# The passage from the output projection to the MLP: turning the first token tile early, with ordered engines

## The chip, the cores and the metric

One NeuronCore of a Trainium2 chip runs the whole program. The metric is the device time of one execution in microseconds, as the median of several runs. The matrix engine (TensorE) appears in the profile as PE for matmuls and PEld for its weight loads, VectorE as DVE, ScalarE as ACT, GpSimd as POOL, and SyncE, which issues most transfers, as SP.

## The reference

The reference is one layer of a transformer-like block on 256 tokens of width 2048. Three mixing branches (two kinds of attention and a recurrent one) are gated, summed and projected; then a two-layer MLP follows. What matters here is the end of the first half and the beginning of the second:

```python
m = g_a * (y_a @ w_branch_a) + g_b * (y_b @ w_branch_b) + g_c * (y_c @ w_branch_c)
x = x + rms_norm(m @ w_out, norm_mix_post)
hdn = square(relu(rms_norm(x, norm_mlp_pre) @ w_mlp_up))      # 2048 -> 8192
x = x + rms_norm(hdn @ w_mlp_down, norm_mlp_post)             # 8192 -> 2048
```

All is in float32 from end to end.

## The kernel before

**Precision by parts.** A float32 product is made of three products of a reduced form: each operand is split into a high part (a rounded copy) and a low part (the rest), and high x high, low x high and high x low are summed in PSUM. A weight tile of 128 x 1024 therefore goes through three stages: a transfer from DRAM into a buffer `raw` (three buffers), a copy by ACT to `whi` (line 144) and a subtraction by DVE to `wlo` (line 145), each with three buffers in the pool `wpool`. `wsplit` does the two operations, `wraw` the transfer, and `wnext` keeps `AHEAD` (one) further weights split ahead in the list `wq`. Activations are packed the same way, high part beside low part, in tiles named `pk` of 128 x 512.

**Token form and column form.** In the output projection the tokens stand on the PSUM partitions. `tok` computes, for one block of 512 output columns, two PSUM tiles, one for each half of the tokens (token tile 0 and 1). It goes through eight weight tiles, which I call steps; a step holds two slices of 128 of the inner dimension and makes six matmuls of 512 columns for each token tile. Its parameter `lag` says for how many of the last steps the second token tile is put off: `prod` computes token tile 0 for those steps first, `tok` hands out the first PSUM tile, and then does the kept steps for token tile 1. In the MLP's first layer the hidden columns stand on the partitions. A unit is 128 hidden columns; it takes two weight tiles (halves), and in each half eight matmuls with the high part of the weight over 512 columns (high and low parts of all 256 tokens) and eight with the low part over 256 columns.

**The passage.** Four column blocks (`for g in range(4)`) of the output projection give `m @ w_out`. Each PSUM tile is squared and summed by ACT (line 888) and multiplied with the norm's gain by DVE (line 886) into `mg`. The fourth block completes the mean square; two small operations on POOL (lines 861 and 862) make the norm's factor `r2` from it, and `add_mixed` (line 878, DVE) adds the scaled result to `x1`. The MLP needs `x1` the other way around: `turned` (line 907) turns it with 128 x 128 transposes on PE, two token tiles side by side in a PSUM tile `mps`, and `split` (lines 225 and 226) makes the 16 packed tiles `upk2`, with the next norm's gain as scale. In the fourth block `lag` is 4. Transposes of token tile 0 come after the last product of token tile 1, a few PSUM tiles ahead of those of token tile 1.

**The MLP.** The hidden dimension is worked in four quarters `q`. For the first, 16 units (`up`) run by themselves. Their results are finished by `post` (copy, add, relu, square) and brought by `forms` to the operands `fm` of the down product, which for the first three quarters is written with seven block products instead of eight (`down`; lines 1069 to 1071 are its three matmuls, line 963 loads its weights into `raw2`, line 1033 adds such weights on DVE and line 1036 by a transfer of POOL's). Units of the next quarter are mixed between these products in a list `work`, which `drive` runs through: it prepares the next item's weights, issues an item's matmuls, and then the posts of the item before.

**What sets the order.** Within a stretch marked with `tc.manual_schedule(engines=...)` the named engines execute their instructions in the order in which the program writes them. Elsewhere a planner that estimates durations orders each engine's instructions before the program runs. In either case each engine runs its own stream in a fixed order, and semaphores hold an instruction until its inputs are there and its buffer is free. In the kernel before, PE alone has a manual stretch, in the mixing branches, which ends ahead of the third gate; the output projection and the MLP are planned. SBUF pools are opened and closed as a stack; a new pool takes over the memory of a closed one as its tiles come free.

Of the kernel before, what the change touches and what calls it, by code (L numbers as in the profile page):

```python
# [17 lines left out]
T = 256  # L18
D = 2048
# [30 lines left out]
def hybrid_block(ctx, tc, xt, x, gains, params, consts, lora, gup, wst, out):  # L50
# [90 lines left out]
    def wsplit(raw):  # L141
        hi = wpool.tile([128, HALF], F32R, tag="whi", name=nm("whi"), bufs=3)
        lo = wpool.tile([128, HALF], F32R, tag="wlo", name=nm("wlo"), bufs=3)
        A.activation(hi, raw, AF.Copy)  # L144
        V.tensor_tensor(lo, raw, hi.bitcast(F32), ALU.subtract)  # L145
# [31 lines left out]
    def tok(pks, lag=1):  # L177
# [31 lines left out]
        for hl, k0 in kept:  # L209
            prod(hl, k0, 1)  # L210
            tick()
        yield ps[1]
# [630 lines left out]

    def fm():
        return p2.tile([128, 7, 128], F32R, tag="fm", name=nm("fm"), bufs=16)

    def gain(n, tiles):

        t = [a.bitcast(F32) for a in tiles]
# [15 lines left out]
    g2, loads = gain(0, [fm().rearrange("p a b -> p (a b)")[:, 0:512] for _ in range(4)])  # L865
# [13 lines left out]

    r2, sum2 = [], []  # L880
    ss2 = cpool.tile([128, 2, 4], F32, name="ss2")
    for g in range(4):
        gs = slice(512 * g, 512 * g + 512)
        for tt, ps in enumerate(tok(mpk, 4 if g == 3 else 1)):
            def gained():
                V.tensor_tensor(mg[tt][:, gs], ps, g2[g], ALU.mult)

            A.activation(junk(), ps, AF.Square, accum_out=ss2[:, tt, g:g + 1])
            if g < 3:
                gained()  # L890
                if g == 2:
                    sum2.append(rstd_of(ss2[:, tt, :], EPS, None))
                continue
            r2.append(rstd_of(ss2[:, tt, :], EPS, sum2[tt]))
            if tt == 0:
                gained()
                for c in range(0, D, 512):
                    add_mixed(0, c, 512)
            else:
                pend = gained  # L900
    upk2 = []
    ss3 = cpool.tile([128, 2, 4], F32, name="ss3")
    trs = []

    def turned(k2, tt):
        for i in range(2):
            PE.transpose(trs[k2 // 2][:, i * T + tt * 128:i * T + tt * 128 + 128],
                         x1[tt][:, (k2 + i) * 128:(k2 + i) * 128 + 128], C("ident"))

    for k2 in range(0, KT, 2):  # L910
        while len(trs) < min(k2 // 2 + 4, 8):
            trs.append(mps())
            turned(2 * len(trs) - 2, 0)
        if k2 == 8:
            pend()
# [388 lines left out]
```

## Time and profile before

| | |
|---|---|
| median of 3 runs | 1560.79 us (1556.21 to 1565.39) |
| profiled execution | 1562.27 us |
| its span, first to last instruction | 1560.5 us |
| mean granted TensorE clock | 0.991 |
| busy: PE, PEld | 98%, 81% of the span |
| busy: DVE, ACT, POOL | 74%, 58%, 6% |
| read from HBM | 279.77 MB, 181 GB/s over the span |
| last output-projection block begins | 829.96 us |
| down products begin | 951.16 us |

The times of a profile are of that one execution, from its first instruction on. Matmuls are pipelined, so the start-to-start distance of weight loads (PEld) tells more of PE's pace than the duration of one matmul. A row of the timeline merges equal instructions that follow one another; a bracket at its end says how long the engine was idle before it and what ended that wait. Idle time of an engine other than PE costs nothing by itself here.

### The profile page before, as it was taken

The numbers are of one execution on the slowest core, as the hardware profiler recorded it, in microseconds if no ns is written. First come the engines' busy times: TensorE is split into PE (matmuls) and PEld (weight loads), VectorE is DVE, ScalarE is ACT, GpSimd is POOL, SyncE is SP. The second block draws the span as 40 slices with busy tenths as digits, with TensorE's granted clock in tenths as the row PEclk, the third lists the DMA queues.
The fourth block names the chain that finished last, engine by engine and source line by source line (L and its number), as shares of the span: only waits on it lengthen the run. The fifth ranks groups of instructions, "written<-read, shape, count | busy, mean of one in ns | idle before, by whom it ended". The sixth has DMA issues, their size and how long they took to land.

```text
span 1560.5 us, 22381 instructions
## 1 busy us (share of the span) xinstructions
PE 1524.2 (98%) x8318; PEld 1265.7 (81%) x8318; DVE 1157.1 (74%) x1566; ACT 907.9 (58%) x1369; POOL 88.5 (6%) x146
## 2 busy tenths in 40 slices
PE   7999999999999999999999999999999999999997
PEld 6888887887887787788887888888888877888885
DVE  7765568896558896645555778789988899888855
ACT  7565367545466554644444766567766676666542
POOL 0030001100001100000000000000000000000000
PEclk9999999999999998999999999999999999999999
DMA  7645554455445553355695557798888888887764
GB/s 242 206 159 176 162 165 150 138 190 189 135 144 179 174 164 96 125 180 188 228 306 164 171 188 201 216 266 254 242 257 250 230 236 239 263 253 232 214 200 136
DMA packets 101197, 308.50 MB, mean 198 GB/s; under 512 B 10080, under 2 KB 12512, under 8 KB 101088
## 3 DMA queue, kind: packets, MB, share of 16 engines
q1 hardware_dynamic: 91344, 280.66, 55.1%
q0 software_dynamic: 6912, 25.17, 8.7%
q8 instruction: 65, 1.06, 0.3%
q10 hardware_dynamic: 2832, 1.24, 0.3%
q14 instruction: 44, 0.36, 0.1%
HBM read 279.77 MB, written 2.10 MB: 181 GB/s over the span
## 4 chain that ended last, share of the span: by engine, by line
PE 66%; issue 10%; DVE 10%; DMA 9%; ACT 4%; POOL 0%; ACTq 0%; SPq 0%; POOLq 0%; DVEq 0%
PE gps L204 27%; PE gps L160 15%; PE gps L164 8%; DMA raw<-raw 5%; PE gps L189 5%; DVE wlo L145 5%; DMA raw<-in_wst_dram 4%; ACT whi L144 2%; PE gps L166 1%; PE mps L1069 1%; PE mps L1071 1%; PE mps L1070 1%; PE gps L1071 1%; PE gps L1069 1%; PE gps L1070 1%
## 5 line engine op out<-in xcount | busy, mean ns | idle before, releaser
L145 DVE TENSOR_TENSOR wlo<-raw,whi 128x1024 fp32r<-128x1024 f32 x590 | 716.1, 1223 | 272.4 <-ACT whi L144 254.4
L144 ACT ACTIVATE whi<-raw 128x1024 fp32r<-128x1024 f32 x590 | 618.2, 1055 | 342.0 <-PE gps L204 153.8
L160 PE MATMUL gps<-pk,whi 128*128 128x512 f32 x1501 | 386.2, 395 | 2.1 <-ACT whi L144 1.0
L160 PEld LDWEIGHTS gps<-pk,whi 128*128 128x128 f32 x1501 | 278.2, 189 | 62.4 <-issue 5.8
L204 PE MATMUL gps<-whi,pk 128*128 128x512 f32 x1144 | 293.8, 395 | 0.4 <-ACT whi L144 0.4
L204 PEld LDWEIGHTS gps<-whi,pk 128*128 128x128 f32 x1144 | 213.5, 189 | 47.0 <-issue 1.3
L164 PEld LDWEIGHTS gps<-pk,wlo 128*128 128x128 f32 x1608 | 220.1, 191 | 16.0 <-DVE wlo L145 0.7
L164 PE MATMUL gps<-pk,wlo 128*128 128x256 f32 x1608 | 225.9, 283 | 0.1
L204 PE MATMUL gps<-wlo,pk 128*128 128x512 f32 x572 | 159.8, 397 | 0.4 <-DVE wlo L145 0.4
L204 PEld LDWEIGHTS gps<-wlo,pk 128*128 128x128 f32 x572 | 107.3, 190 | 24.2 <-DVE wlo L145 1.1
L991 ACT ACTIVATE tmp<-gps 128x256 f32<-128x256 f32 x64 | 24.6, 384 | 90.7 <-PE gps L166 90.7
L1069 PE MATMUL mps<-whi,fm 128*128 128x512 f32 x192 | 76.1, 396 | 0.8 <-ACT whi L144 0.7
L1071 PE MATMUL mps<-wlo,fm 128*128 128x512 f32 x192 | 75.5, 393 | 0.4 <-DVE wlo L145 0.2
L1070 PE MATMUL mps<-whi,fm 128*128 128x512 f32 x192 | 75.0, 391 | 0.0
L1036 POOL DMA_DIRECT2D raw<-raw x48 | 41.9, 873 | 554.2 <-DVE raw L1033 313.2
L189 PE MATMUL gps<-whi,pk 128*128 128x512 f32 x264 | 71.3, 393 | 0.0
L1071 PE MATMUL gps<-wlo,fm 128*128 128x512 f32 x144 | 57.2, 397 | 2.4 <-DVE wlo L145 2.1
L1033 DVE TENSOR_TENSOR raw<-raw,raw 128x1024 f32<-128x1024 f32 x48 | 58.7, 1223 | 1.0
L189 PEld LDWEIGHTS gps<-whi,pk 128*128 128x128 f32 x264 | 49.2, 188 | 11.2 <-issue 0.7
L1069 PE MATMUL gps<-whi,fm 128*128 128x512 f32 x144 | 56.8, 395 | 1.4 <-ACT whi L144 1.4
L1070 PE MATMUL gps<-whi,fm 128*128 128x512 f32 x144 | 56.5, 392 | 0.0
L204 PE MATMUL gps<-whi,fm 128*128 128x512 f32 x208 | 51.4, 389 | 0.0
(294 smaller groups left out, 1551.7 us busy)
## 6 DMA issues: line engine op xcount, KB each, us to landing
raw<-in_wst_dram SPq DMA_DIRECT2D x518, 512.0 KB, 4.4
raw<-raw POOLq DMA_DIRECT2D x48, 512.0 KB, 6.7
x<-in_x_dram SPq DMA_DIRECT2D x8, 256.0 KB, 6.5
out_dram<-x SPq DMA_DIRECT2D x8, 256.0 KB, 2.8
x<-in_xt_dram SPq DMA_DIRECT2D x3, 512.0 KB, 7.3
fm<-in_gains_dram SPq DMA_DIRECT2D x4, 256.0 KB, 5.5
pk<-in_gains_dram SPq DMA_DIRECT2D x4, 256.0 KB, 4.5
con<-in_consts_dram SPq DMA_DIRECT2D x1, 576.0 KB, 7.8
```

Source lines behind the costliest of these rows:

```text
L144: A.activation(hi, raw, AF.Copy)
L145: V.tensor_tensor(lo, raw, hi.bitcast(F32), ALU.subtract)
L160: PE.matmul(ps, hi[:, i * 128:i * 128 + 128], pks[i], start=first and i == 0, stop=False)
L164: PE.matmul(ps[:, 0:T], lo[:, i * 128:i * 128 + 128], pks[i][:, 0:T], start=False, stop=False)
L189: PE.matmul(ps[tt], pks[k][:, c:c + 128], w[:, (k - k0) * 512:(k - k0) * 512 + 512], start=k == 0 and part == 0 and w is hl[0], stop=w is ...
L204: PE.matmul(ps[tt], pks[k][:, c:c + 128], w[:, (k - k0) * 512:(k - k0) * 512 + 512], start=k == 0 and part == 0 and w is hl[0], stop=False)
L991: A.activation(b, ps[0][:, T:2 * T], AF.Copy)
L1033: V.tensor_tensor(R[a], R[a], R[b], ALU.add)
L1036: G.dma_start(out=R[a], in_=R[b], accum_op=ALU.add)
L1069: PE.matmul(Q[f], a, w, start=d == 0 and i == 0, stop=False)
L1070: PE.matmul(Q[f], b, w, start=False, stop=False)
L1071: PE.matmul(Q[f], a, wl, start=False, stop=d == 3 and i == 1)
```

## The change

It has five parts.

1. Token tile 0 is turned early. In the fourth block `lag` goes from 4 to 6, and `tok` takes a list `mid` of functions to call between the kept steps of token tile 1. After the fourth of the six, two PSUM tiles of token tile 0 are turned and cut (`early`), after the fifth a third, after the sixth the last.
2. Token tile 0's share of three units. The six weights of the units 0 to 2 are split ahead into `uw`. `part` does the matmuls with the high weight parts for one token tile alone, high and low tokens in one matmul as two runs of 128 columns; `rest` does those with the low weight parts for both. Token tile 0's parts stand before and between the transposes of token tile 1.
3. More split weights ahead. The lookahead grows block by block (`ahead` 1, 3, 6, 9), up to the six weights of `uw` (`top`). From the eighth step on most split weights go into a pool `op` of 18 further tiles `kw`; the pool closes after the three units, and only then the pool `p3` (for `fm`, `raw2` and `sfm`) opens. `raw` keeps its three buffers.
4. Order. From the fourth block to the end of the first quarter's units PE, ACT, DVE and POOL run in written order; PE alone does so from there to the last down product's beginning.
5. Token tile 1's gain multiplication follows directly on its square, and `add_mixed` works on 512 columns for it as well. `cut` splits 128 columns at a time. The MLP's squares for its second norm go from the units 0 to 7 to the units 4 to 11.

```diff
-    def wsplit(raw):
-        hi = wpool.tile([128, HALF], F32R, tag="whi", name=nm("whi"), bufs=3)
-        lo = wpool.tile([128, HALF], F32R, tag="wlo", name=nm("wlo"), bufs=3)
+    def wsplit(raw, n=None):
+        hl = home[0](n) if home[0] else None
+        hi, lo = hl or (wpool.tile([128, HALF], F32R, tag=t, name=nm(t), bufs=3) for t in ("whi", "wlo"))
...
-        while len(wq) < 1 + AHEAD and wpos[0] < wst.shape[0]:
-            wsplit(wraw())
+        while len(wq) < 1 + ahead[0] and wpos[0] < top[0]:
+            wsplit(wraw(), wpos[0] - 1)
...
-        for hl, k0 in kept:
+        for i, (hl, k0) in enumerate(kept):
             prod(hl, k0, 1)
             tick()
+            if i < len(mid):
+                mid[i]()
...
+    def roomy(n):
+        if n - wo < 8 or (n - wo) % 12 < 3:
+            return None
+        return [op.tile([128, HALF], F32R, tag="kw", name=nm("kw"), bufs=18) for _ in range(2)]
+
+    home[0], top[0] = roomy, wo + 38
...
+    def turn(tt, b):
+        trs[tt, b] = mps()
+        for i in range(4):
+            PE.transpose(trs[tt, b][:, 128 * i:128 * i + 128],
+                         x1[tt][:, 512 * b + 128 * i:512 * b + 128 * i + 128], C("ident"))
...
+    def part(j, half, tt):
+        for i in range(8):
+            o, u = (t.rearrange("p (a t) -> p a t", a=2)[:, :, 128 * tt:128 * tt + 128] for t in (gp[j], upk2[8 * half + i]))
+            PE.matmul(o, uw[2 * j + half][0][:, i * 128:i * 128 + 128], u, start=tt == half == i == 0, stop=False,
+                      skip_group_check=True)
...
+    mid = [lambda: None] * 3 + [lambda: early(0, 1), lambda: early(2)]
+    order = tc.manual_schedule(engines={mybir.EngineType.PE, mybir.EngineType.Activation, mybir.EngineType.DVE, mybir.EngineType.Pool})
     for g in range(4):
...
+        if g == 3:
+            order.__enter__()
+        for tt, ps in enumerate(tok(mpk, 6, mid) if g == 3 else tok(mpk)):
             A.activation(junk(), ps, AF.Square, accum_out=ss2[:, tt, g:g + 1])
+            if g == 3:
+                r2.append(rstd_of(ss2[:, tt, :], EPS, sum2[tt]))
+            V.tensor_tensor(mg[tt][:, gs], ps, g2[g], ALU.mult)
...
+            if g == 3 and tt == 0:
                 for c in range(0, D, 512):
                     add_mixed(0, c, 512)
+        ahead[0] = (3, 6, 9, AHEAD)[g]
+    uw = [wq.pop(0) for _ in range(6)]
+    gp = [gps() for _ in range(3)]
+    home[0], top[0] = None, wst.shape[0]
+    early(3)
+    for j in range(3):
+        part(j, 0, 0)
+    for b in range(4):
+        add_mixed(1, 512 * b, 512)
+    part(0, 1, 0)
+    turn(1, 0)
+    part(1, 1, 0)
+    turn(1, 1)
+    cut(1, 0, 1)
+    turn(1, 2)
+    part(2, 1, 0)
+    turn(1, 3)
+    cut(1, 2, 3)
+    for _ in range(1 + AHEAD):
+        wsplit(wraw())
...
-    for j in range(KT):
+    for j in range(3):
+        rest(j, 0)
+    for half in range(2):
+        for j in range(3):
+            part(j, half, 1)
+            if half:
+                rest(j, 1)
+                hidden(0, j, gp[j])
+    po.close()
...
+    forms(0, 0)
+    for j in range(3, KT):
         work.extend(up(0, j))
...
     drive()
+    order.__exit__(None, None, None)
+    order = tc.manual_schedule(engines={mybir.EngineType.PE})
+    order.__enter__()
```

`early(b, ...)` turns the named quarters of token tile 0 and cuts them; `cut` copies with the gain as scale on ACT (all high parts first) and subtracts on DVE; `hidden` is the old `post` under a new name.

More of the change, by code (lines that the diff above doesn't have):

```diff
@@ L863, in rstd_of @@
         return r
-    g2, loads = gain(0, [fm().rearrange("p a b -> p (a b)")[:, 0:512] for _ in range(4)])
+    g2, loads = gain(0, [op.tile([128, 512], F32, name=nm("g2")) for _ in range(4)])
     x1 = [p2.tile([128, D], F32, tag="x1", name=nm("x1"), bufs=2) for _ in range(2)]
@@ new lines, in cut @@
+    def cut(tt, *bs):
+        for low in range(2):
+            for b in bs:
+                for i in range(4):
+                    k = 4 * b + i
+                    if len(upk2) == k:
+                        upk2.append(pk())
+                    hi, lo = (upk2[k][:, c + 128 * tt:c + 128 * tt + 128] for c in (0, T))
+                    src = trs[tt, b][:, 128 * i:128 * i + 128]
+                    if low:
+                        V.scalar_tensor_tensor(lo, src, P("g3", k), hi.bitcast(F32), ALU.mult, ALU.subtract)
+                    else:
+                        A.activation(hi, src, AF.Copy, scale=P("g3", k))
@@ new lines, in part, with rest @@
+    def part(j, half, tt):
[3 more added lines that the diff above has]
+                      skip_group_check=True)
+    def rest(j, half):
+        for i in range(8):
+            PE.matmul(gp[j][:, 0:T], uw[2 * j + half][1][:, i * 128:i * 128 + 128], upk2[8 * half + i][:, 0:T],
+                      start=False, stop=half == 1 and i == 7, skip_group_check=True)
@@ L897, in hybrid_block @@
+            if g == 2:
+                sum2.append(rstd_of(ss2[:, tt, :], EPS, None))
+            if g == 3 and tt == 0:
                 for c in range(0, D, 512):
                     add_mixed(0, c, 512)
-            else:
-                pend = gained
-    upk2 = []
-    ss3 = cpool.tile([128, 2, 4], F32, name="ss3")
[L903 to L915, printed above, removed]
-        add_mixed(1, 128 * k2, 256)
-        turned(k2, 1)
-        for i in range(2):
-            u = pk()
-            split(trs[k2 // 2][:, i * T:i * T + T], u, P("g3", k2 + i))
-            upk2.append(u)
+        ahead[0] = (3, 6, 9, AHEAD)[g]
+    assert len(wq) == 6
+    uw = [wq.pop(0) for _ in range(6)]
@@ L976, in hybrid_block, with hidden @@
     hid, fmh, fml = {}, {}, {}
+    def hidden(q, j, ps):
+        b, t = tmp(), tmp()
+        A.activation(b, ps[:, T:2 * T], AF.Copy)
+        V.tensor_tensor(t, ps[:, 0:T], b, ALU.add)
+        A.activation(t, t, AF.Relu)
+        if j % 2 == 0:
+            hid[q, j // 2] = pk().bitcast(F32).rearrange("p (s t) -> p s t", s=4)
+        h = hid[q, j // 2]
+        A.activation(h[:, 0:4:3] if j % 2 == 0 else h[:, 1:3], t.rearrange("p (s t) -> p s t", s=2), AF.Square)
+        if q == 0 and 4 <= j < 12:
+            A.activation(junk(), x1[j % 2][:, 512 * (j // 2 - 2):512 * (j // 2 - 2) + 512], AF.Square,
+                         accum_out=ss3[:, j % 2, j // 2 - 2:j // 2 - 1])
+        if q == 0 and j in (12, 13):
+            e = cpool.tile([128, 2], F32, name=nm("eps4"))
+            V.tensor_reduce(e[:, 0:1], ss3[:, j % 2, :], AX.X, ALU.add)
+            V.tensor_scalar(e[:, 0:1], e[:, 0:1], 1.0 / D, EPS, ALU.mult, ALU.add)
+            V.tensor_tensor(e[:, 1:2], e[:, 0:1], e[:, 0:1], ALU.mult)
+            V.tensor_scalar(e[:, 1:2], e[:, 1:2], EPS, None, ALU.mult)
+            eps4.append(e[:, 1:2])
     def up(q, j):
@@ L1153, in hybrid_block @@
     drive()
+    order.__exit__(None, None, None)
     hp = [hp[k] for k in range(KT)]
```

58 lines of the change are left out of this document (20 added, 38 removed).

## The prediction

> **What bounds the kernel now.** I read the page first, then the table of windows around the passage, then the timeline there. In the windows the columns after the stretch are its length, the busy time of PE, PEld, DVE, ACT and POOL with counts, the granted clock, the DMA share and GB/s.
>
> ```profile
> PE 1524.2 (98%) x8318; PEld 1265.7 (81%) x8318; DVE 1157.1 (74%) x1566; ACT 907.9 (58%) x1369; POOL 88.5 (6%) x146
> 829.96:846.28 16.32, 16.32 (x73) 13.51 (x72) 7.64 (x11) 5.88 (x8) 0.00 (x0) 1.00 0.58 194
> 846.28:852.57 6.29, 6.06 (x26) 4.38 (x25) 3.90 (x5) 4.46 (x6) 1.42 (x2) 1.00 0.30 101
> 852.57:878.54 25.97, 23.18 (x128) 18.50 (x129) 21.96 (x46) 19.48 (x47) 1.37 (x2) 0.93 0.37 118
> 857.46:860.87 3.41, 2.91 (x9) 2.03 (x10) 3.37 (x9) 3.41 (x11) 0.00 (x0) 0.50 0.01 2
> 951.16:1461.66 510.50, 504.31 (x2546) 422.53 (x2545) 448.77 (x511) 337.40 (x469) 41.20 (x48) 1.00 0.84 243
> ```
>
> TensorE bounds nearly everything: it is busy 1524.2 of 1560.5 us. So an edit is worth only the holes that it closes in PE's stream. The passage has some: in 852.57 to 878.54 PE is busy for 23.18 of 25.97 us at a mean clock of 0.93, and the 3.41 us from 857.46 ran at 0.50. These three windows hold all that the turning edits can win. The later window, the down products, is the other place that the edit touches.
>
> The next rows, of the timeline, give start and duration; a bracket is idle time and what ended it.
>
> ```profile
> 764.12 0.42 PEld L835 LDWEIGHTS mps<-ident,m 128*128 128x128 f32 x4 [0.40 <-PE gps L189]
> 764.51 1.46 PEld L204 LDWEIGHTS gps<-whi,pk 128*128 128x128 f32 x7
> ...
> 829.96 1.77 PEld L204 LDWEIGHTS gps<-whi,pk 128*128 128x128 f32 x8
> 832.68 1.77 PEld L204 LDWEIGHTS gps<-whi,pk 128*128 128x128 f32 x8
> 840.84 0.87 PEld L189 LDWEIGHTS gps<-whi,pk 128*128 128x128 f32 x4
> ...
> 849.39 0.60 ACT L888 ACTIVATE junk<-gps 128x512 f32<-128x512 f32 x1 [0.72 <-PE gps L189]
> 851.13 0.56 POOL L862 TENSOR_TENSOR rs<-rs,cst 128x1 f32<-128x1 f32 x1
> 851.72 2.74 DVE L878 SCALAR_TENSOR_TENSOR x<-mg,rs,x 128x512 f32<-128x512 f32 x4 [0.21 <-POOL rs L862]
> 852.54 0.42 PEld L907 LDWEIGHTS mps<-ident,x 128*128 128x128 f32 x4 [0.62 <-PE gps L189]
> 853.69 0.82 POOL L861 TENSOR_SCALAR rs<-ss,ssum 128x1 f32<-128x1 f32 x1 [2.01 <-ACT junk L888]
> 855.18 1.67 DVE L878 SCALAR_TENSOR_TENSOR x<-mg,rs,x 128x256 f32<-128x256 f32 x4 [0.72 <-POOL rs L862]
> 855.72 1.62 PE L907 MATMUL mps<-ident,x 128*128 128x128 f32 x8 [1.88 <-DVE x L878]
> ...
> 878.53 1.80 PEld L160 LDWEIGHTS gps<-pk,whi 128*128 128x128 f32 x8
> 884.12 1.80 PEld L160 LDWEIGHTS gps<-pk,whi 128*128 128x128 f32 x8
> ```
>
> A full output-projection step is 832.68 - 829.96 = 2.72 us (12 matmuls, 0.227 each), half a step (one token tile) 1.36. Four transposes take 764.51 - 764.12 = 0.39. An MLP unit takes 884.12 - 878.53 = 5.59, so its 16 narrow matmuls (256 columns) take (5.59 - 16 x 0.227) / 16 = 0.123 each. From the square of a finished tile (849.39) over POOL's two operations and the adds to the first transpose (852.54) is 3.15 us. In the old order the second tile's chain has little beside it: PE waits 1.88 us for its add.
>
> **The change part by part.** Passage: unit 3 starts at 878.53. The last column block (g == 3) starts at 829.96. Without holes it needs 8 x 2.72 = 21.8 us, the 32 transposes 8 x 0.39 = 3.1 and three units 16.8: 871.6. The old holes and the slow clock are therefore 6.9 us together.
>
> The new order adds PE work: in `part`, 48 wide matmuls become 96 narrow ones, 96 x 0.123 - 48 x 0.227 = 0.9 us. No row has a matmul whose columns lie in two runs of 128. I take the contiguous narrow price, the nearest row; if each cost half a wide one (0.114) nothing would be added, and at a wide one's price 10.9. Ideal end 872.5, **at most 6.0 us won**.
>
> Does tile 0 arrive in time? Step 24 and 25 run whole and six steps for tile 0 alone, so tile 0 ends at 829.96 + 5.44 + 8.16 = 843.6. Four half steps of tile 1 carry PE to 849.0. Its chain of 3.15 would give the first transpose at 846.9, 2.1 us early. But ACT now runs in written order, and `tok` has written the splits of weights 30 to 37 ahead of tile 0's square. All eight must land first. That supply decides:
>
> ```profile
> L144 ACT ACTIVATE whi<-raw x14: 1059/1061/1063, 811.4 to 847.6; 128x1024 fp32r<-128x1024 f32 x14
> L145 DVE TENSOR_TENSOR wlo<-raw,whi x15: 1224/1226/1228, 809.9 to 849.7; 128x1024 fp32r<-128x1024 f32 x15
> DMA to landing us min/median/max: 3.2/4.2/5.2
> ...
> 787.42 0.43 SPq L963 DMA_DIRECT2D raw<-in_wst_dram  x1
> 797.56 1.06 ACT L144 ACTIVATE whi<-raw 128x1024 fp32r<-128x1024 f32 x1 [0.20 <-DMA raw<-in_wst_dram]
> 808.64 0.43 SPq L963 DMA_DIRECT2D raw<-in_wst_dram  x1
> 829.93 1.06 ACT L144 ACTIVATE whi<-raw 128x1024 fp32r<-128x1024 f32 x1 [0.22 <-PE gps L189]
> ```
>
> `raw` still has three buffers. A buffer is held from issue to landing (median 4.2 in 811 to 850), through whi (1.06) and wlo (1.23): 6.5 us for three loads, 2.16 each, whatever number of kw buffers follows. That is faster than PE eats whole steps (2.72), slower than half steps (1.36). Steps from 0: whi at 829.93 waited for PE to finish step 23, whose buffer it takes, so it is step 26; twelve splits earlier, 797.56 is step 14, which waited on its load. From there the ring runs freely: step 37 is 23 loads later, 797.6 + 23 x 2.16 = 847.3, its whi ends at 848.4. Square and chain then give the first transpose at 848.4 + 3.15 = 851.5, against PE free at 849.0: a hole of 2.5, and 0.3 more as the second chunk's add (2.74 / 4 = 0.69) outlasts its four transposes. So **2.8 us of stall**. Bounds from the landings: at 3.2 a cycle is 5.5, whi ends at 840.8, no stall; at 5.2 a cycle is 7.5, whi ends at 856.2, stall 10.7. I take the median's row. The old loads of the down weights (L963, 787.42 to 808.64) leave this stretch, since their pool now opens later; they are wanted only from 951 and cost nothing there.
>
> The old half clock at 857.46 followed a hole of 1.88; the new one is longer, so I count one: 3.41 x 0.5 = 1.7 us. Passage: 6.0 - 2.8 - 1.7 = **1.5 us won**. The Trainium skill, "TensorE: Matmul & The Clock Gate", section "Part 1: The HAM clock gate", says that an idle window of some 3.4 us drops PE to half rate; here the stretch at 0.50 is 3.41 us long, but the hole was shorter than that window. By the page's words a hole of 2.8 would cost no clock, and the passage would win 3.2, a case inside the forecast's own range.
>
> Behind that, little is late. Tile 1's chain, 3.15 plus four new `cut` subtractions ahead of its adds, has `turn(0,3)` and 32 narrow matmuls beside it (0.39 + 32 x 0.123 = 4.3).
>
> ```profile
> L225 ACT ACTIVATE pk<-mps,par 128x256 fp32r<-128x256 f32 x16 | 6.8, 472 | 4.5 <-DVE pk L226 2.5 <-PE mps L907 2.0
> L226 DVE SCALAR_TENSOR_TENSOR pk<-mps,par,pk 128x256 fp32r<-128x256 f32 x16 | 7.1, 478 | 0.6 <-ACT pk L225 0.5
> L1016 DVE TENSOR_TENSOR sfm<-pk,sfm 128x128 f32<-128x128 f32 x3 | 0.9, 289 | 0.1
> ```
>
> `cut` makes 32 operations of 128 columns per engine instead of 16 of 256. At the nearest small row (0.289) that is 32 x 0.289 - 16 x 0.478 = 1.6 us more on DVE and about the same on ACT, between nothing and the full 7.6; it lies under the 17.5 us of the three units. If that cover went, all 1.6 would show. In the rest of the units DVE and ACT now follow written order too:
>
> ```profile
> 878.54:951.16 72.62, 72.62 (x419) 63.91 (x417) 51.67 (x76) 45.85 (x78) 0.71 (x1) 1.00 0.60 189
> ```
>
> They are busy 51.67 and 45.85 of 72.62 us there, PE all of it; I cost that order at nothing.
>
> Down products, now with PE in written order:
>
> ```profile
> 951.16 0.19 PEld L1069 LDWEIGHTS gps<-whi,fm 128*128 128x128 f32 x1
> 1295.81 0.19 PEld L1069 LDWEIGHTS gps<-whi,fm 128*128 128x128 f32 x1 [1.84 <-ACT whi L144]
> 1300.44 0.19 PEld L1069 LDWEIGHTS mps<-whi,fm 128*128 128x128 f32 x1 [0.39 <-ACT whi L144]
> 1335.42 0.19 PEld L1069 LDWEIGHTS gps<-whi,fm 128*128 128x128 f32 x1
> 1356.12 0.19 PEld L1069 LDWEIGHTS gps<-whi,fm 128*128 128x128 f32 x1
> 1461.88 1.09 PEld L204 LDWEIGHTS gps<-whi,fm 128*128 128x128 f32 x5
> ```
>
> A clean group of seven products and two units takes 1356.12 - 1335.42 = 20.70 us. Twenty-four take 496.8; the stage takes 1461.88 - 951.16 = 510.7. So 13.9 us are holes, mostly PE waiting for splits (1.84 at 1295.81). Around 1300 the planner has put products out of written order, a first matmul of one (mps) between two of another (gps). Written order undoes that; it makes no split earlier. Bounds: all 13.9 won, or as much lost again, since the timing of every stage behind shifts. I take 1.5 won, nearest to the two waits at the reordered place (1.84 + 0.39).
>
> Sum: 1.5 + 1.5 = 3.0. The profiled execution took 1562.27 (1560.5 of span and 1.8 around it), so 1559.3; the median of runs shown is 1.5 lower: **1558**.
>
> **The rivals.**
>
> 1. The loads keep up: at a cycle of 5.5 there is neither stall nor half clock, 6.0 + 1.5 won, 1553.3. For it stand the shortest landing of 3.2 and the six loads that leave; against it the median with about as much traffic. The Trainium skill, "DMA: Bandwidth & Descriptors", section "Anatomy of one DMA", gives 2.0 us plus bytes over 436 GB/s, which is an estimate of 3.2 for 512 KB. That agrees with the shortest landing, not the median; by it this rival comes true.
>
> 2. Slower: the in-order wait. ACT holds tile 0's square behind whi 37, at PE's `turn(0,0)`. With stall and half clock it eats the 6.0 us when whi 37 ends after 849.9, a landing of about 4.4. At 5.2 it is 10.7 + 1.7 - 6.0 = 6.4 slower, and the rest unchanged: 1567.2. For it: every square, gain and add that hits a ready split lengthens the cycle. Against: only the longest landings reach it.
>
> 3. Written order cures more of the down stage: 8 of 13.9 us, 1551.3. Against: its waits are for splits, which PE's order doesn't move.
>
> 4. The first down product's split stays behind the last written posts: copy, add, relu, square and five operations of the forms, nine at about 0.4 (between 0.289 and 0.478), and a whi of 1.06, a hole of 4.7 us at 951: 1562.5. Against it these rows: matmuls of the gate written after the ordered block stand among the block's own.
>
> ```profile
> 627.53 0.57 PE L692 MATMUL mps<-SC,Xt 128*64 128x64 f32 x12
> 628.03 1.19 PE L204 MATMUL gps<-whi,pk 128*128 128x512 f32 x4
> 629.29 1.03 PE L718 MATMUL mps<-gn,con 128*128 128x256 f32 x4
> ```
>
> L204 there belongs to the gate that is written after L692 and L718, so later work is let in between.
>
> 5. It doesn't do what it says: PE or ACT is late elsewhere and tile 0 is turned no earlier; then only the 0.9 us remain: 1561.7.
>
> **How the numbers follow.** Forecast 0.42 (1555 to 1562); loads keep up 0.20 (1551 to 1556); in-order wait 0.15 (1563 to 1570); down stage cured 0.13 (1548 to 1553); late split or no effect 0.10 (1560 to 1565). Half a percent, 7.8 us, is about what a measurement of this kernel can tell from no change. Below 1553.0 lie nearly all of the cured case (0.12) and about a third of the second (0.07): 0.19. Above 1568.6 lies a part of the in-order case: 0.07. The range 1551 to 1567 leaves out about 2 in 10.
>
> **What would show it.** The square after tile 0 starting right behind step 37's whi, and PE idle at `turn(0,0)` for 2 to 3 us: forecast. No idle there and no 0.5 clock: rival 1. Landings near 5 and a hole of 8 or more: rival 2. Unit 3 should start about 1.5 us earlier, counted from the last block's start. The down stage's length against 510.7 shows rivals 3 and 4. Wrong would be, above all, a two-run matmul slower than 0.123 us, or splits in another order than written.

## The result, and the profile after

The changed kernel takes 1573.09 us (median of 5 runs, 1568.32 to 1575.15) against 1560.79 for the kernel before (5 runs, 1556.21 to 1565.39): the ratio is 1.0065, with a 95% interval of 1.004 to 1.0089. The forecast was 1558 with a range to 1567, so it missed, and on the wrong side. The profiled execution took 1575.15 us. Of the twelve executions of e4 further down, one took 5320.20 us; its median there is that of the other eleven.

First the page's row of busy times, then the windows of the changed kernel; the columns are those of the prediction (length; busy PE, PEld, DVE, ACT, POOL; clock; DMA share; GB/s).

```profile
PE 1526.1 (97%) x8366; PEld 1266.9 (81%) x8366; DVE 1160.3 (74%) x1578; ACT 910.9 (58%) x1385; POOL 85.4 (5%) x146
```

```profile
829.57:877.58 48.01, 44.70 (x274) 39.81 (x273) 32.38 (x62) 25.03 (x58) 2.09 (x4) 0.96 0.45 144
853.75:857.17 3.42, 3.42 (x12) 2.73 (x11) 2.57 (x9) 1.75 (x8) 0.00 (x0) 0.50 0.08 31
877.58:953.23 75.65, 73.61 (x419) 63.82 (x417) 52.52 (x83) 52.29 (x96) 0.00 (x0) 1.00 0.62 207
953.23:1474.76 521.53, 507.95 (x2547) 421.81 (x2546) 449.85 (x513) 336.98 (x469) 41.92 (x48) 1.00 0.82 238
```

PE is busy 1.9 us longer than before (1526.1 against 1524.2), but the span grew by 12.9 (1573.4 against 1560.5): the change has opened holes. The windows say where. The first is the **passage**, from the start of the last projection block to unit 3: 48.01 us, where the old kernel took 878.53 - 829.96 = 48.57. The third holds **units 3 to 15**: 75.65 against 72.62, though their matmuls are the same. The fourth is the **down stage**: 521.53 against 510.7. All else differs by less than half a microsecond.

**The passage** stalled as forecast. This is its timeline (start, duration, engine, operation; a bracket is idle time and what ended it):

```profile
847.08 1.06 ACT L147 ACTIVATE whi<-raw 128x1024 fp32r<-128x1024 f32 x1 [1.73 <-DMA raw<-in_wst_dram]
...
848.36 1.06 ACT L147 ACTIVATE whi<-raw 128x1024 fp32r<-128x1024 f32 x1 [0.22 <-DMA raw<-in_wst_dram]
849.32 0.58 ACT L946 ACTIVATE junk<-gps 128x512 f32<-128x512 f32 x1
...
851.48 2.74 DVE L882 SCALAR_TENSOR_TENSOR x<-mg,rs,x 128x512 f32<-128x512 f32 x4 [0.21 <-POOL rs L866]
...
852.29 1.32 PE L902 MATMUL mps<-ident,x 128*128 128x128 f32 x8 [3.30 <-DVE x L882]
```

The square of token tile 0 (L946, old L888) has no bracket: it had been ready and stood in ACT's queue behind the split of step 37, which waited for its transfer. PE was free at 852.29 - 3.30 = 848.99 and sat idle for 3.30 us (2.8 forecast). The row at 0.50 in the windows is the half clock that was counted. The loads landed as taken:

```profile
DMA to landing us min/median/max: 3.3/4.3/4.6
```

**Units 3 to 15** were costed at nothing. Here is ACT in the middle of that stretch, after and then before; behind it one of PE's weight loads of the changed kernel, and the sum of all such waits there (total us, times, longest):

```profile
920.50 0.42 ACT L1038 ACTIVATE tmp<-tmp 128x256 f32<-128x256 f32 x1 [1.55 <-DVE tmp L1037]
920.95 0.42 ACT L1042 ACTIVATE pk<-tmp 128x256 f32<-128x256 f32 x1
921.27 0.61 ACT L1044 ACTIVATE junk<-x 128x512 f32<-128x512 f32 x1
...
921.88 0.51 ACT L1075 ACTIVATE fm<-pk 128x384 fp32r<-128x384 f32 x1
922.51 0.63 ACT L1076 ACTIVATE fm<-sfm 128x512 fp32r<-128x512 f32 x1
923.04 2.00 ACT L147 ACTIVATE whi<-raw 128x1024 fp32r<-128x1024 f32 x2
```

```profile
918.35 1.05 ACT L144 ACTIVATE whi<-raw 128x1024 fp32r<-128x1024 f32 x1
919.30 0.41 ACT L993 ACTIVATE tmp<-tmp 128x256 f32<-128x256 f32 x1
919.74 0.42 ACT L997 ACTIVATE pk<-tmp 128x256 f32<-128x256 f32 x1
920.06 1.04 ACT L144 ACTIVATE whi<-raw 128x1024 fp32r<-128x1024 f32 x1
921.01 0.51 ACT L1019 ACTIVATE fm<-pk 128x384 fp32r<-128x384 f32 x1
```

```profile
912.60 1.69 PEld L163 LDWEIGHTS gps<-pk,whi 128*128 128x128 f32 x8 [1.13 <-ACT whi L147]
```

```profile
PEld gps L163 <- ACT whi L147: 3.3, 4, 1.3
```

Before, the planner let a split in after every two or three steps of the post-processing. After, a unit's whole tail (relu and square of the hidden values, the moved square of L1044, two operations of the forms) runs first, and the next two splits come together behind it. On every second unit from 900 us on, four times in all, PE arrives first; before, its weight loads waited for no split in this stretch. ACT is busy for no more than 52.29 of the 75.65 us: it is late, not full. The Trainium skill, "Perfetto Trace Analysis", section "Tensor Engine Instruction (MATMUL, LD_WEIGHTS)", calls ACT, DVE and GPSIMD strict first-in first-out queues. These rows agree: the split at 923.04 waited behind other instructions of its own engine although its load had landed at 919.36, and until 920.50 ACT itself was idle, held by a relu that waited for DVE. The loads of all four splits that PE waited for had landed 3.7 to 4.1 us before the splits began.

**The down stage** lost the most in this execution. The waits of PE's weight loads in it (total us, times, longest), first after, then before:

```profile
PEld gps L1127 <- DVE wlo L148: 19.0, 24, 1.7
PEld mps L1127 <- DVE wlo L148: 6.4, 11, 1.0
...
PEld gps L167 <- DVE wlo L148: 0.7, 1, 0.7
PEld mps L1125 <- ACT whi L147: 0.3, 1, 0.3
```

```profile
PEld gps L1071 <- DVE wlo L145: 6.3, 10, 1.0
...
PEld mps L1069 <- ACT whi L144: 2.8, 5, 1.1
PEld gps L1069 <- ACT whi L144: 2.6, 4, 1.8
PEld mps L1071 <- DVE wlo L145: 2.4, 5, 0.7
```

L1127 is the old L1071, the product with the low part of a weight, the last thing that a split makes. Its waits went from 8.7 to 25.4 us. The first product of a weight (old L1069, now L1125), which needs the high part alone, went the other way, from 5.4 to 0.3. The order accounts for both. These are weight loads around one wait for a low part, before and then after:

```profile
1291.20 1.77 PEld L160 LDWEIGHTS gps<-pk,whi 128*128 128x128 f32 x8
1293.20 0.19 PEld L1071 LDWEIGHTS gps<-wlo,fm 128*128 128x128 f32 x1 [0.22 <-DVE wlo L145]
```

```profile
1303.81 0.19 PEld L1127 LDWEIGHTS gps<-wlo,fm 128*128 128x128 f32 x1 [1.69 <-DVE wlo L148]
...
1304.63 1.81 PEld L163 LDWEIGHTS gps<-pk,whi 128*128 128x128 f32 x8
```

The planner put eight ready matmuls of a unit between a product's high part and its low part, and they covered most of the wait for DVE. In written order such a unit stands behind the product. For the high part it had done the reverse: the first product at 1295.81, a row of the prediction, stood ahead of a unit's ready matmuls and waited 1.84 us. Of the 336 matmuls with a low part in the stage, 7 or 8 stand right behind a unit's matmul in every kernel of this study with that order planned, and none in those with it written. Several executions, further down, show how much of the 10.8 us belongs to the order and how much to the execution.

### The profile page after: what moved, and what is told of

It reads as the page before. It is cut to its first block, busy times and chain, and to the rows that moved or that the text cites. A ratio compares the mean times of both kernels' runs of the same rounds, so it can differ in the third digit from the quotient of the medians.

```text
span 1573.4 us, 22526 instructions
## 1 busy us (share of the span) xinstructions
PE 1526.1 (97%) x8366; PEld 1266.9 (81%) x8366; DVE 1160.3 (74%) x1578; ACT 910.9 (58%) x1385; POOL 85.4 (5%) x146
## 4 chain that ended last, share of the span: by engine, by line
PE 62%; issue 12%; DVE 10%; DMA 10%; ACT 5%; POOL 0%; ACTq 0%; DVEq 0%; POOLq 0%; SPq 0%
PE gps L207 26%; PE gps L163 12%; PE gps L167 7%; DMA raw<-in_wst_dram 6%; PE gps L192 5%; DVE wlo L148 5%; DMA raw<-raw 4%; ACT whi L147 2%; PE gps L1127 1%; PE mps L1125 1%; DVE y L1132 1%; PE mps L1127 1%; PE gps L169 1%; PE mps L1126 1%; PE gps L924 1%
## 5 line engine op out<-in xcount | busy, mean ns | idle before, releaser
L148 DVE TENSOR_TENSOR wlo<-raw,whi 128x1024 fp32r<-128x1024 f32 x568 | 688.1, 1222 | 263.7 <-ACT whi L147 248.9
L147 ACT ACTIVATE whi<-raw 128x1024 fp32r<-128x1024 f32 x568 | 594.0, 1055 | 332.0 <-PE gps L207 140.2
L163 PE MATMUL gps<-pk,whi 128*128 128x512 f32 x1456 | 372.5, 394 | 4.7 <-ACT whi L147 2.8
L163 PEld LDWEIGHTS gps<-pk,whi 128*128 128x128 f32 x1456 | 269.2, 188 | 64.4 <-issue 6.0
L207 PE MATMUL gps<-whi,pk 128*128 128x512 f32 x1040 | 267.5, 395 | 0.4 <-ACT whi L147 0.4
L207 PEld LDWEIGHTS gps<-whi,pk 128*128 128x128 f32 x1040 | 193.6, 188 | 42.7 <-issue 1.3
L167 PEld LDWEIGHTS gps<-pk,wlo 128*128 128x128 f32 x1560 | 213.0, 190 | 16.4 <-DVE wlo L148 1.4
L167 PE MATMUL gps<-pk,wlo 128*128 128x256 f32 x1560 | 218.7, 282 | 0.3 <-DVE wlo L148 0.3
L207 PE MATMUL gps<-wlo,pk 128*128 128x512 f32 x520 | 145.6, 397 | 0.4 <-DVE wlo L148 0.4
L207 PEld LDWEIGHTS gps<-wlo,pk 128*128 128x128 f32 x520 | 97.4, 190 | 22.1 <-DVE wlo L148 1.1
L1127 PE MATMUL mps<-wlo,fm 128*128 128x512 f32 x192 | 76.2, 397 | 2.1 <-DVE wlo L148 1.9
L1125 PE MATMUL mps<-whi,fm 128*128 128x512 f32 x192 | 75.7, 394 | 0.0
L1127 PE MATMUL gps<-wlo,fm 128*128 128x512 f32 x144 | 58.9, 409 | 9.5 <-DVE wlo L148 9.0
L192 PE MATMUL gps<-whi,pk 128*128 128x512 f32 x224 | 60.7, 393 | 0.0
L1125 PE MATMUL gps<-whi,fm 128*128 128x512 f32 x144 | 56.5, 393 | 0.0
L192 PEld LDWEIGHTS gps<-whi,pk 128*128 128x128 f32 x224 | 41.7, 188 | 9.4 <-issue 0.7
```

Source lines behind the costliest of these rows:

```text
L163: PE.matmul(ps, hi[:, i * 128:i * 128 + 128], pks[i], start=first and i == 0, stop=False)
L167: PE.matmul(ps[:, 0:T], lo[:, i * 128:i * 128 + 128], pks[i][:, 0:T], start=False, stop=False)
L192: PE.matmul(ps[tt], pks[k][:, c:c + 128], w[:, (k - k0) * 512:(k - k0) * 512 + 512], start=k == 0 and part == 0 and w is hl[0], stop=w is ...
L207: PE.matmul(ps[tt], pks[k][:, c:c + 128], w[:, (k - k0) * 512:(k - k0) * 512 + 512], start=k == 0 and part == 0 and w is hl[0], stop=False)
L1125: PE.matmul(Q[f], a, w, start=d == 0 and i == 0, stop=False)
L1127: PE.matmul(Q[f], a, wl, start=False, stop=d == 3 and i == 1)
```

## The experiments

Stages are in us, from the profiled execution of each kernel: the passage, units 3 to 15, the down stage. "Ratio" is to the kernel before, from runs on the same chip, with its 95% interval. "Written" and "planned" say how the order was set: in units 3 to 15 that of ACT, DVE and POOL, in the down stage that of PE.

| kernel | passage | units | down | median | ratio |
|---|---|---|---|---|---|
| before | 48.57 | 72.63 planned | 510.72 planned | 1560.79 | 1 |
| before_again | 49.18 | 72.63 planned | 514.78 planned | 1566.50, one run | |
| after | 48.01 | 75.65 written | 521.53 written | 1573.09 | 1.0065 (1.004 to 1.0089) |
| after_again | 47.60 | 76.31 written | 510.71 written | 1559.73, one run | |
| e1_down_planned | 49.62 | 76.41 written | 509.35 planned | 1567.8 | 1.0032 (1.0011 to 1.0053) |
| e2_before_down_written | 49.19 | 72.63 planned | 514.66 written | 1564.66 | 1.0026 (1.0005 to 1.0046) |
| e3_square_first | 47.16 | 77.35 written | 517.32 written | 1569.96 | 1.0046 (1.003 to 1.0061) |
| e4_units_planned | 49.82 | 72.52 planned | 512.17 written | 1565.92 | 1.0037 (1.0017 to 1.0057) |
| e6_before_layout | 48.56 | 72.63 planned | 508.83 planned | 1560.95 | 0.9985 (0.9966 to 1.0003) |
| e7_raw4 | 42.68 | 76.51 written | 517.82 written | 1567.92 | 1.0058 (1.0035 to 1.0081) |
| e8_best | 42.68 | 72.52 planned | 511.59 planned | 1566.05 | 1.0033 (1.0016 to 1.0051) |
| e9_late_two | 44.61 | 75.12 written | 521.41 written | 1568.71 | 1.0047 (1.0027 to 1.0066) |
| e10_late_combo | 44.59 | 72.52 planned | 514.41 planned | 1561.88 | 1.0005 (0.999 to 1.002) |
| e11_raw4_late | 42.68 | 72.52 planned | 511.37 planned | 1558.55 | 0.9979 (0.996 to 0.9998) |
| e11_again | 42.68 | 72.52 planned | 520.86 planned | 1556.92 | 0.9976 (0.9962 to 0.999) |
| e12_raw4_down_written | 42.71 | 72.52 planned | 514.47 written | 1561.36 | 1.0001 (0.9987 to 1.0016) |
| e13_raw4_units_written | 42.68 | 75.65 written | 510.00 planned | 1562.15 | 1.001 (0.999 to 1.003) |

**The down stage: PE's order, or the new addresses?** e1 takes the second manual stretch out of the changed kernel; e2 puts it, alone, into the kernel before; e6 gives the kernel before about the memory layout of the changed one (`fm`, `raw2` and `sfm` in a pool of their own).

```diff
     drive()
     order.__exit__(None, None, None)
-    order = tc.manual_schedule(engines={mybir.EngineType.PE})
-    order.__enter__()
     ys.extend(
...
-    order.__exit__(None, None, None)
     hp = [hp[k] for k in range(KT)]
```

Above is e1's edit of the changed kernel. e2's is the same three lines, put into the kernel before at the same two places. That of e6, of the kernel before:

```diff
+    p3 = ctx.enter_context(tc.tile_pool(name="p3", bufs=1))
...
-        return p2.tile([128, 7, 128], F32R, tag="fm", name=nm("fm"), bufs=16)
+        return p3.tile([128, 7, 128], F32R, tag="fm", name=nm("fm"), bufs=16)
...
-        raw = p2.tile([128, HALF], F32, tag="raw2", name=nm("raw"), bufs=6)
+        raw = p3.tile([128, HALF], F32, tag="raw2", name=nm("raw"), bufs=6)
...
-        s = p2.tile([128, 4, 128], F32, tag="sfm", name=nm("sfm"), bufs=1)
+        s = p3.tile([128, 4, 128], F32, tag="sfm", name=nm("sfm"), bufs=1)
```

> The changed kernel without the second ordered stretch: PE in the down products is planned again. Its down stage (first down matmul to the first matmul of the last projection) took 521.3 us against 510.7 before. Theory O (PE's written order costs it): the stage returns to 511, the time to about 1562. Theory L (where the tiles lie in SBUF now that their pool opens later) and theory P (the stage starts from another state): the stage stays at 521, the time at 1573.

> The kernel before with PE in written order from the end of the first quarter's units to the last projection, nothing else. Theory O: the down stage goes from 511 to 521 us, the time from 1561 to about 1572. Theories L and P: the stage stays at 511, the time at 1561.

> The kernel before with fm and the weights of the down products in a pool of their own behind x1, y and junk, so that they lie at about the addresses of the changed kernel; the order of every engine is that of before. Theory L: down stage 521 us, time about 1571. Theories O and P: 511 and 1561.

e6 is no slower than before (0.9966 to 1.0003): the layout is out. e2 is slower by the order alone, and e1 gets 5.3 us of the changed kernel's loss back (the two medians were not measured beside each other, and the intervals of the two ratios overlap). So the order costs in the down stage, though less than the first profile's 10.8.

**The passage: is it ACT's queue?** e3, made from the changed kernel, writes the splits of steps 34 to 37 behind token tile 0's square, gain and adds.

```diff
-    home[0], top[0] = roomy, wo + 38
+    home[0], top[0] = roomy, wo + 34
...
                     add_mixed(0, c, 512)
+                top[0] = wo + 38
+                while wpos[0] < top[0]:
+                    wsplit(wraw(), wpos[0] - 1)
```

> The changed kernel with the splits of weights 34 to 37 written behind the square, gain and adds of token tile 0 instead of ahead of them. If the in-order wait is the passage's stall (PE idle 3.3 us at the first transpose, then 3.4 us of half clock), both go: from the last block's first matmul to unit 3's first falls from 47.9 to about 43 us, the time from 1573 to about 1568. Rival: the adds or POOL are late by themselves; then a stall of 2 to 3 us stays and the stretch is 47 or more.

The timeline of e3:

```profile
847.62 1.03 PE L902 MATMUL mps<-ident,x 128*128 128x128 f32 x8
...
851.55 1.06 ACT L147 ACTIVATE whi<-raw 128x1024 fp32r<-128x1024 f32 x1 [5.59 <-DMA raw<-in_wst_dram]
...
852.52 3.18 ACT L918 ACTIVATE pk<-mps,par 128x128 fp32r<-128x128 f32 x12
...
854.19 4.16 PE L924 MATMUL gps<-pk,kw 128*128 128x256 f32 x16 [1.89 <-DVE pk L916]
```

The transposes start without a wait, but the hole has moved on: now `cut` (L918) stands behind the split of step 37, and the first `part` (L924) waits 1.89 us and meets half clock. The wait belongs to the late split, wherever it is written ahead of something urgent. e9, also from the changed kernel, writes only the splits 36 and 37 late, behind the last cuts, where `part` for the third unit is the first to want them.

```diff
-    home[0], top[0] = roomy, wo + 38
+    home[0], top[0] = roomy, wo + 36
...
+    early(3)
+    for _ in range(2):
+        wsplit(wraw(), wpos[0] - 1)
     uw = [wq.pop(0) for _ in range(6)]
...
-    early(3)
```

> The changed kernel with splits 36 and 37 alone written behind the first tile's last cuts (in the run before, splits 34 to 37 stood behind the first tile's adds, and the cuts then waited behind split 37). Theory B: the hole is nothing but ScalarE's order, the first tile's square behind splits whose loads land late: the square runs at about 846, the first transposes are no more than 0.5 us late, the cuts follow them at once, splits 36 and 37 come in time for the third unit: passage 43.5 to 45, no half clock ahead of 870, time 1573.1 less 3.5 = 1569.5. Rival: the wait moves on a second time, now to the third unit's products at splits 36 and 37: a hole of 1 to 2 us there with 3.4 us of half clock behind it, passage 46.5 to 48, time 1572.

```profile
841.99 0.58 ACT L946 ACTIVATE junk<-gps 128x512 f32<-128x512 f32 x1
...
846.83 1.04 PE L902 MATMUL mps<-ident,x 128*128 128x128 f32 x8
...
853.91 1.22 PE L924 MATMUL gps<-pk,whi 128*128 128x256 f32 x8 [0.47 <-ACT whi L147]
```

The passage falls from 48.01 to 44.61, with no half clock in it. The order was the wait's place; is the supply its cause? e7 keeps the order of the changed kernel and gives every fourth load of that stretch a fourth buffer. The memory comes from the squares' dead output, which then has one buffer there; `v` of the down stage, which shared those two, keeps two.

```diff
-        raw = wpool.tile([128, HALF], F32, tag="raw", name=nm("raw"), bufs=3)
+        raw = extra[0].tile([128, HALF], F32, tag="raw4", name=nm("raw"), bufs=1) if extra and wpos[0] % 4 == 3 else wpool.tile([128, HALF], F32, tag="raw", name=nm("raw"), bufs=3)
...
-    home[0], top[0] = roomy, wo + 38
+    home[0], top[0], extra[:] = roomy, wo + 38, [op]
...
-        return p2.tile([128, 512], F32, tag="junk", name=nm("junk"), bufs=2)
+        return p2.tile([128, 512], F32, tag="junk", name=nm("junk"), bufs=1)
```

> The changed kernel with a fourth buffer for weight loads while the early units' weights are being fetched (a second buffer for the squares' dead output pays for it). Theory R: three buffers set the supply, 6.5 us for a load's cycle by 3 = 2.16; with four 1.63, so split 37 ends about 5 us earlier, the 3.3 us hole ahead of the first transposes goes, and the 3.4 us of half clock behind it: passage 43 to 44 in place of 48.0, time 1573.1 less 4.5 = 1568.5. Rival D: four loads in flight share what three had, each lands in 5.5 to 6 us instead of 4.2 and the rate stays about 2.1 per load: passage 47.5 to 48.5, time 1573.

Passage 42.68: the supply of three buffers was the cause, and with a fourth neither hole nor half clock is left. Four loads in flight slow one another only a little (median 4.7 us to landing against 4.3 with three): in e11, which has the same passage, the landings of 811 to 850 us are

```profile
DMA to landing us min/median/max: 3.1/4.7/6.1
```

so the ring is (4.7 + 1.06 + 1.23) / 4 = 1.75 us for each load. The passage is 5.9 us under the old one, where the prediction's ideal was 6.0. But e7 also lost something earlier; its weight loads on PE show where:

```profile
764.84 0.88 PEld L207 LDWEIGHTS gps<-wlo,pk 128*128 128x128 f32 x4
769.00 1.91 PEld L207 LDWEIGHTS gps<-whi,pk 128*128 128x128 f32 x8 [3.28 <-ACT whi L147]
```

I read this as the first load into the fourth buffer waiting for memory that the stage before had not yet left, with the loads behind it in SP's queue; e11 below tests that.

**Units 3 to 15.** e4 lets ACT, DVE and POOL out of the written order behind the three early units; PE keeps it.

```diff
     forms(0, 0)
+    order.__exit__(None, None, None)
+    order = tc.manual_schedule(engines={mybir.EngineType.PE})
+    order.__enter__()
     for j in range(3, KT):
```

> The changed kernel, but ScalarE, VectorE and GpSimd are taken out of the written order behind the three early units (TensorE keeps it). Theory U: the 3.0 us that units 3 to 15 lost (72.63 to 75.65) come from the written order of ScalarE and VectorE, where a unit's post-processing and the moved squares stand ahead of the next split: the stretch goes back to 72.6, the passage stays 48.0 within 0.6, the down stage between 515 and 522, time 3 us under the changed kernel's median of 1573.1, so 1570. Rival: the stretch is longer because of what the passage leaves behind (four splits made late, the clock), then it stays at 75 to 77 and the time at 1573.

```profile
876.08:948.60 72.52, 72.52 (x418) 63.85 (x417) 51.90 (x75) 46.44 (x80) 0.72 (x1) 1.00 0.67 218
```

PE has no hole left in the stretch, in the window above as in every other kernel with that order planned (72.52 to 72.63); with it written, all took 75.12 to 77.35. The passage, which the edit leaves as it is, did not stay within the 0.6 us expected: it took 49.82, behind a hole of 4.27 us and 6.83 us of half clock.

**Putting it together.** e8 is e7 with the edits of e4 and e1. e10 has e9's late splits in place of the fourth buffer. e11 is e8 with the fourth buffer used only from the sixteenth load on (the condition gains `wpos[0] >= wo + 16`), when its memory has long been free.

> The changed kernel with the fourth load buffer, units 3 to 15 in the planner's order and the down stage in the planner's order: all that is left of the change is the early share itself. If theories R, U and O hold together: 829.6 to the last block, passage 43.5, units 72.6, down stage 509.5, rest 98.6, span 1553.8, time 1555.5, under the kernel before (1560.8) by 5. If the fourth buffer gives nothing: 1560, no difference from before. If the planner's order saves only what the medians of the runs so far say (5.3 us): 1560 with the buffer's gain, 1565 without it.

> Splits 36 and 37 late, units 3 to 15 and the down stage in the planner's order. By the stages that the runs so far show: 829.6 to the last block (826 to 834 from one execution to the next), passage 44.6, units 72.6, down stage 510 (508.8 to 511.6 in four executions of planned order), rest 98.6: span 1555.4, time 1557, under the kernel before (1561) by 4. If the stages add up but the executions' medians do not (the kernel with the fourth buffer and both planner's orders had 1560.6 in its profiled execution and a median of 1566): 1561 to 1566, no faster than before.

> As the kernel with the fourth load buffer and both planner's orders, but the fourth buffer is used only from the sixteenth load on, when its memory has been free for long: in the two kernels with that buffer the last block began at 833.1 and 833.4, behind a hole of 3.5 us at 765.5 and 3.4 us of half clock at 770, since a load waited for the memory of the stage ahead. Theory: without that hole the last block begins at 829.6 again, within 4; passage 42.7, units 72.5, down stage 510, rest 98.6: span 1553.4, time 1555. If the hole stays, 1559 in the profile.

e8's stages are as hoped, except that its last block starts 3.5 us late behind the hole seen in e7, and its median is 1566. The last blocks of e8 and e11 begin 5.2 us apart (833.42 and 828.19), their medians lie 7.5 apart on two chips; the rest is not explained. Without that hole e11 is faster than before: 0.9979 and, measured again, 0.9976, some 3.5 us. Both intervals end below 1, and it is the fastest kernel of the study. Its windows:

```profile
828.19:870.87 42.68, 42.68 (x274) 38.70 (x272) 30.80 (x68) 28.36 (x70) 2.02 (x4) 1.00 0.37 126
870.87:943.39 72.52, 72.52 (x419) 63.84 (x417) 51.91 (x75) 46.37 (x80) 0.72 (x1) 1.00 0.66 218
943.39:1454.76 511.37, 504.64 (x2547) 422.56 (x2546) 449.69 (x512) 337.22 (x469) 41.26 (x48) 1.00 0.83 243
```

In the first two PE is busy for the whole of the length. e10 comes to no difference from before (0.999 to 1.002), though its passage is 4.0 us shorter; its one profile, with 514.41 in the down stage, can't say where the gain went.

**How much is order, how much the execution?** The two kernels were profiled again, unaltered; and e11 was run beside itself with one of the two orders written again (e12: the down stage; e13: the units; each is e11 without the edit of e1 or of e4).

> The changed kernel, unaltered, for a second profiled execution, to see how far its stages repeat. If the stages belong to the kernel: passage 48.0 and units 3 to 15 75.65, each within 0.3, down stage 521 within 1. If the down stage varies by execution, as 512.2 to 521.5 in the six kernels with TensorE in written order suggest: passage and units as before, down stage anywhere from 512 to 522, with the waits of the down products for wlo going the same way (16 to 25 us).

> The kernel before, unaltered, for a second profiled execution. If the stages belong to the kernel: passage 48.57, units 72.63 within 0.1, down stage 510.7 within 1. If the down stage varies by execution in planned order too (508.8 to 514.4 in six kernels): passage and units the same, down stage anywhere from 508 to 515.

> The kernel with the fourth load buffer used late and units and down stage planned, once more, as the ground of the next two. If its gain was real: ratio to the kernel before 0.996 to 1.000 (0.9979 the first time), median near 1558.5, passage 42.7, units 72.5, down stage 509 to 515. If the first time was luck: ratio 1.000 to 1.004.

> The same kernel with TensorE in written order through the down stage. Theory O (that order costs in every execution, 4 to 5 us as two pairs of medians say): 4 to 5 us slower than the kernel above in the same call, 1563. Rival: the first profile's 521.5 was one execution's misfortune and the order costs nothing: within 2 us of the kernel above. The profile's own down stage may fall anywhere from 510 to 522.

> The same kernel with ScalarE, VectorE and GpSimd in written order through units 3 to 15, the down stage planned. Theory U: that stretch 75.6 to 77.4 as in all seven executions so far with that order, against 72.5, so 3 to 5 us slower than the first kernel of this call, 1562. Rival: with no waits in the passage the splits are further ahead and the stretch loses less than 1.5 us: 1559.5.

In these pairs the passage and the units repeat to within 0.7 us. Over more kernels the passage does not: with the changed kernel's passage unaltered it took 48.01 and 47.60, but 49.62 in e1 and 49.82 in e4, the hole being 2.91 to 4.27 us long and the half clock behind it 3.41 or 6.83. With the old passage it took 48.56 to 49.19, four times too (before, before_again, e2, e6). The means are 48.76 and 48.88, so the change won next to nothing there. The down stage varies most: 521.53 and 510.71 in the changed kernel, 511.37 and 520.86 in e11. So one profile cannot price an order there, and the 10.8 us of the first reading were partly chance. What repeats are the waits for the split. The rows are of after_again (written), e12 (written) and e11_raw4_late (planned):

```profile
PEld gps L1127 <- DVE wlo L148: 12.8, 16, 1.7
PEld mps L1127 <- DVE wlo L148: 1.6, 4, 0.5
```

```profile
PEld gps L1127 <- DVE wlo L148: 13.8, 17, 1.7
PEld mps L1127 <- DVE wlo L148: 3.9, 8, 1.0
```

```profile
PEld gps L1127 <- DVE wlo L148: 5.3, 11, 1.0
PEld mps L1127 <- DVE wlo L148: 4.6, 9, 0.9
```

On the `gps` tiles this wait is 12.8 us or more in every execution with PE's order written, and 9.1 or less in every one with it planned. That is not the net loss, for written order takes waits for `whi` away: all waits of the weight loads for splits together are 15.1 to 26.4 us in the eight executions with the order written (mean 20.6) and 13.0 to 23.3 in the nine with it planned (mean 16.6). The means of the stage itself are 516.3 and 512.4, 3.8 apart. The medians of the runs give nearly the same price: e12 is 1561.36 - 1556.92 = 4.4 us slower than e11 measured beside it, e2 3.9 slower than before, e1 5.3 faster than after. (The intervals of e12 and e11 just meet, at 0.9987 and 0.999.) For the units, e13 is 1562.15 - 1556.92 = 5.2 slower, with 3.1 of it in the stretch itself (75.65 - 72.52); the intervals of the two ratios, 0.9962 to 0.999 and 0.999 to 1.003, leave room for 3.1.

## Why the prediction was wrong

By its own steps:

- **"At most 6.0 us won" in the passage** was right: 5.9 with a fourth buffer. The price of 0.123 us for a matmul over two runs of 128 columns held: in e11 the weight loads of `part` follow one another at 0.12 us, and the transposes and all `part` matmuls run without a hole in a passage of 42.68 us, against 872.5 - 829.96 = 42.5 computed.
- **"2.8 us of stall"** and the half clock were right in mechanism and place: 3.30 us, then 3.42 us at 0.50. The Trainium skill's rule ("TensorE: Matmul & The Clock Gate", "Part 1: The HAM clock gate"), by which such a hole would cost no clock, did not hold here. The sizes were luck in part: with the same passage e1 and e4 had holes of 3.90 and 4.27 us and twice the half clock. The 1.5 us to be won were 0.6 in the first pair of profiles, 1.6 in the second and 0.1 in the means of four against four. (Two sums have slips on which nothing rests: 843.6 + 3.15 is 846.75, not 846.9, and three units with the added 0.9 us are 17.7, not 17.5.) Rival 1 fell with the landings (median 4.3), and with them the estimate of 3.2 us: the Trainium skill's fit ("DMA: Bandwidth & Descriptors", "Anatomy of one DMA — SWDGE (gpsimd) path") is of transfers that GpSimd issues, and SP issues these loads. Rival 2 asked for median landings above 4.4 and was not needed.
- **"I cost that order at nothing"** is the step that failed first. It rested on shares: DVE busy 51.67 and ACT 45.85 of 72.62 us. Shares say that the work fits; they do not say that a split is there in time when it stands behind a unit's whole tail. Price: 3.0 us in the profile, 3.1 to 5.2 by e13.
- **"I take 1.5 won"** in the down stage is the step that failed most, and in sign. Half of its reason came true: the waits at first products, such as the 1.84 and 0.39 us that it set out to win, went from 5.4 to 0.3 us. What it left out is what stands between the products: the planner's order covered waits for `wlo` with ready matmuls of the units, written order does not, and these waits went from 8.7 to 25.4 us in the first pair of profiles. Net, written order costs 3.8 us in the means of the stage and 4.4 in the medians of e12 and e11. The step had itself bounded the loss at 13.9; then the rivals gave a cure of 8 us a chance of 0.13 and a loss there none, and no case but rival 2 reached above 1565.
- Rival 4, a hole of 4.7 us at the first down product, fell: between 937 and 1037 us of the changed kernel PE has no hole of 0.6 us or more. Rival 5 fell with the transposes, which do run early.

The sum by the runs: the passage wins 0.1 to 0.6, the units cost 3.1 to 5.2, the down stage 4.4, together 6.9 to 9.5 us lost. Measured were 0.0065 x 1561 = 10.1, between 6.2 and 13.9. What is missing to 10.1 lies within the interval and is not explained further. It was not settled which part of e1's edit does the work in the down stage: besides PE's own order, the planner then also placed two splits on ACT and two loads on SP differently.

## What to carry to other kernels

An engine that is busy two thirds of the time can still be the bound of a stretch in written order: look at what stands ahead of each urgent instruction on its engine, above all ahead of the split or copy that feeds PE, before an order is costed at nothing. If an order by hand is needed for one passage, end it with the passage; here each stretch kept longer cost 3 to 5 us. And where several buffers hold a stream, work out the ring (landing plus both uses, over the number of buffers) against the consumer's fastest pace: one buffer more was worth 5.3 us in the passage, more than the better of the two reorderings tried there (48.01 - 44.61 = 3.4).

## What the runs showed of the hardware

**Short holes cost clock.** In the 17 profiles of this study, from 100 to 1545 us, all 56 holes of PE between 0.9 and 1.45 us were followed by full clock. Of 45 holes of 1.88 to 4.3 us, 38 had a stretch at 0.50 starting near them, 3.4 us long or a whole number of such lengths (up to 23.9); the other 7, of 1.98 to 2.24 us and all near 661 us, had none. So no hole up to 1.44 us cost clock here, and from 1.88 us on, well under the 3.4 us of one stretch, most did; no hole in between was seen, and the holes of the two groups lie, but for two, at different places of the program. A stretch near 185 us, in six of the executions, follows no such hole at all.

**One stage varies by ten microseconds from one execution to the next.** The two executions of e11 (1555.20 and 1564.58 us) differ by 9.4, and their down stages by 9.5. The row is that of the second, in the windows:

```profile
943.30:1464.16 520.86, 508.19 (x2547) 421.67 (x2546) 449.02 (x512) 336.59 (x469) 41.24 (x48) 1.00 0.83 238
```

DVE's and ACT's busy times are those of the first to within 0.7 us; what differs in the lists of transfers is how long they took to land, 5.6 against 6.0 us in the median for the weight loads, and more for POOL's copies from buffer to buffer:

```profile
raw<-raw POOLq DMA_DIRECT2D x48, 512.0 KB, 6.3
```

```profile
raw<-raw POOLq DMA_DIRECT2D x48, 512.0 KB, 7.1
```

The first row is of the shorter execution, the second of the longer one. Over all 17 profiles the five stages of 517 us and more have medians of 6.6 to 7.1 for these copies, the twelve shorter ones 6.1 to 6.7. Whether late landings make the stage long, or a long stage only shows them, no run here tells.
